# Output projection in the banks of the attention scores, with its buffers and raw weights in other places and half of its first tile among the last heads

## The chip, the core and the metric

The kernel runs on one core of a Trainium2 chip. TensorE multiplies matrices and transposes, and writes only to PSUM, which has 8 banks of 2 KB in each of 128 partitions. VectorE and ScalarE read PSUM; GpSimd works in the on-chip memory (SBUF). Loads are issued by SyncE, most stores by ScalarE. Each engine runs its own instructions in order and waits for the others by semaphores. The metric is device time in microseconds (us).

## The reference

One transformer layer over 256 prompt tokens and 1024 sample tokens of width 1024. Half of the mixing is latent attention with 8 heads, half is attention in a window of the token grid. Both halves are normalised, concatenated and projected; a gated feed-forward part follows.

```python
def encoder_layer(x, ...):
    h = rmsnorm(x, attn_norm_g)
    proj = h @ w_in
    a = mla_group(proj[..., :o1], proj[..., o1:o2], proj[..., o2:o3], ...)
    b = na_group(proj[..., o3:], na_rpb)
    mix = jnp.concatenate([rmsnorm(a, mla_out_g), rmsnorm(b, na_out_g)], axis=-1)
    x = x + mix @ w_o
    h2 = rmsnorm(x, ffn_norm_g)
    x = x + (jax.nn.silu(h2 @ w_gate) * (h2 @ w_up)) @ w_down
    return x
```

All data is fp32. A product is made of three matmuls on numbers split into a high and a low half (`mm3`, lines 108 to 112: L110 high by high, L111 high by low, L112 low by high).

## The kernel before

The 1280 tokens (prompt first) are ten tiles of 128. The stages follow one another: input projection and window attention (to about 360 us), latent attention (to about 688 us), output projection (to about 823 us), the feed-forward products (lines 915 to 1053) and the down projection (from line 1064).

**Latent attention.** `attend` (line 653) is called for four pairs of heads; in a pair the order is the first 256 sample tokens, the prompt, and then the other three blocks of 256 sample tokens (lines 720 to 730). For each head of a block there are two score groups S (L110 to L112) into one of two PSUM tiles of two banks (`s_tile`, in the pools ppa and ppb). VectorE takes the maximum (L681), ScalarE the exponential (L683) into `ex`, TensorE transposes it into `tp` (L689), ScalarE and VectorE split that into a high and a low half, PT (L99, L100), and TensorE multiplies with the values into `o` (L699). `o` is copied to `os` (L703), transposed (L707), copied to `ob` (L709), and GpSimd adds and scales it into `at` (L712, L714), which ScalarE's queue stores to `a_d` (L717). The tiles tp and o have two banks each, in the pool pp.

**Output projection.** Eight pieces of w_o are loaded through the buffers `m` (three of 4 KB), scaled by GpSimd with the gain `gm` (L762) and split into `wo0` to `wo7` (L94, L96). `mix_in(t)` loads a tile of both attention outputs into `m` and the residual into `x`; ScalarE sums the squares (L779), GpSimd scales (L783), and TensorE transposes in two groups of four into one bank, `trm` (L790), which ScalarE and VectorE split into `mT` (L99, L100). `out_proj` makes two halves of 512 columns, 24 matmuls each, into `po`, and VectorE adds each half to x (L801). `ffn_in` stores x, normalises it (L808, L811), transposes it into `trh` or `trm` (L820) and fills the operands of the next stage.

**What sets the order.** The loop at line 897 asks for tile t + 1 before it projects tile t. Loads are queued on SyncE in the order of the program (line 79), so one that waits holds up those behind it. On the other engines the framework lays down the order when the kernel is built, from a simulated run; `tc.issue_after(ins)` puts the instructions of its block behind `ins` on their engine. At line 898 it holds all of tile t + 1's preparation behind the last high half of tile t's mT. Pools are stacks: those of a later stage lie over those that an earlier one has given back, and each tile waits for the tiles that lay in its place. Here that is:

```python
    for nm in ("lc", "lw", "ke", "kp", "qp", "p2", "qA", "lv0"):
    ...
    for x in reversed(lstack):
        x.release()
    ...
    rw, rm, rxm, rt = r3 = [pool(nm) for nm in ("r3w", "r3m", "r3x", "r3t")]
    po = pool("po", space=PSUM)
```

lc holds the latents (cT, 51,200 bytes per partition), lw small weights (13,312), ke and kp the keys of even pairs and of the prompt (16,384 and 4,096), qp the prompt's queries (4,096), and p2 the small tiles of `attend`, `at` first. r3w holds wo (65,536), r3m the three m and small tiles, r3x two x of 4,096, r3t two mT of 8,192. The PSUM pools pp and po begin at bank 0; ppb lies behind pp and ppa at the other end.

Of the kernel before, what the change touches and what calls it, by code (L numbers as in the profile page):

```python
# [11 lines left out]
F32 = mybir.dt.float32  # L12
# [27 lines left out]
def encoder_trunk(ctx: ExitStack, tc: tile.TileContext, x_tm, x_T, g_attn, w_c, w_v, w_qk,  # L40
# [471 lines left out]
    s_count, last_split = [0], [None]  # L512
# [140 lines left out]
    def attend(p, Q, K, c_lo, c_hi, sample, between=None):  # L653
# [6 lines left out]
        for c in range(c_lo, c_hi):  # L660
            at = p2.tile([P, 2, P], F32, name="at", bufs=2)
            for i in range(2):
# [42 lines left out]
                for u in range(2):  # L705
                    us = slice(u * P, (u + 1) * P)
                    nc.tensor.transpose(op[:, us], os_[:, us], ident)  # L707
# [5 lines left out]
                                        op=ALU.add)  # L713
                nc.gpsimd.tensor_tensor(out=at[:, :, i * DH:(i + 1) * DH], in0=ob[:, :, 0],  # L714
# [36 lines left out]
    rw, rm, rxm, rt = r3 = [pool(nm) for nm in ("r3w", "r3m", "r3x", "r3t")]  # L751
    po = pool("po", space=PSUM)
    gm = rm.tile([P, KC], F32, name="gm")
    gf = rm.tile([P, KC], F32, name="gf")
    load(gm, g_mix)
    load(gf, g_ffn)
    wo = []
    for kc in range(KC):
        raw = rm.tile([P, D], F32, name="m", bufs=3)
        load(raw, w_o[kc])  # L760
        wt = rw.tile([P, 2, D], F32R, name=f"wo{kc}")
        nc.gpsimd.tensor_scalar(out=raw, in0=raw, scalar1=gm[:, kc:kc + 1], scalar2=1.0,  # L762
                                op0=ALU.mult, op1=ALU.mult)
        split_w(wt[:, 0], wt[:, 1], raw)
        wo.append(wt)

    def mix_in(t):
# [4 lines left out]
        x = rxm.tile([P, D], F32, name="x", bufs=2)  # L772
        load(x, x_tm[ts_, :])
# [7 lines left out]
        for i in range(2):  # L781
            hs = slice(i * 512, (i + 1) * 512)
            nc.gpsimd.tensor_scalar(out=mn[:, hs], in0=mx[:, hs], scalar1=r[:, i:i + 1],  # L783
                                    scalar2=1.0, op0=ALU.mult, op1=ALU.mult)
        mT = rt.tile([P, 2, KC, P], F32R, name="mT", bufs=2)
# [6 lines left out]
        return mT, x  # L792

    def out_proj(t, mT, x):
        for hf in range(2):
            hs = slice(hf * 512, (hf + 1) * 512)
            ps = po.tile([P, 512], F32, name="po", bufs=2)
            for kc in range(KC):
                last = mm3(ps, mT[:, 0, kc], mT[:, 1, kc], wo[kc][:, 0, hs], wo[kc][:, 1, hs],
                           kc == 0, kc == KC - 1)  # L800
# [93 lines left out]
    pm = [pool("pm0", space=PSUM, side="right")]  # L894
    cur = mix_in(0)
    A0, w0 = ({}, {}), {}
    for t in range(NT):
        with tc.issue_after(last_split[0]):
            nxt = mix_in(t + 1) if t + 1 < NT else None
        if t == 6:  # L900
            for m, i, b in ((1, 0, "11"), (2, 0, "12"), (1, 1, "11")):
                A0[i][b] = load_A(i, 0, b)
                w0[m, i] = operand(A0[i], m)
        if t == 7:
            A0[1]["12"] = load_A(1, 0, "12")
        last_mm = out_proj(t, *cur)
# [411 lines left out]
```

## Time and profile before

| | us |
|---|---|
| median of three runs | 1643.68 (1642.41 to 1643.81) |
| the profiled execution | 1647.12 |
| its span, first to last instruction | 1645.3 |
| TensorE busy in it | 1594.9 |
| VectorE, ScalarE, GpSimd busy | 884.6, 715.5, 660.4 |

The profile is of one execution, recorded on the chip. Engines are called PE (TensorE), PEld (its weight loads), DVE (VectorE), ACT (ScalarE), POOL (GpSimd) and SP (SyncE); SPq and ACTq are the queues that issue DMAs. L801 is line 801 of the kernel. In a timeline a row gives the start, the duration, the engine, the line, the operation, what it writes and reads, how many were merged, and in brackets the engine's idle time before and what ended it. A matmul's duration overlaps with the next one's, so a rate is read from the starts. PEclk is the granted clock of TensorE, 1.00 being full.

### The profile page before, as it was taken

What the parts mean: (1) busy time and instruction counts of PE and PEld (TensorE: products, weight loads), DVE (VectorE), ACT (ScalarE), POOL (GpSimd) and SP (SyncE); (2) the same over time, 40 slices, a digit from 0 to 9 for tenths busy, and PEclk for the clock granted to TensorE, in tenths of its full rate; (3) what the DMA queues carried; (4) which work ended last, traced back from release to release, by engine and by line L of the source; (5) the groups of instructions that cost most, each with busy time, mean ns of one, the idle gap of its engine ahead of it and who ended that gap; (6) DMA issues with size and microseconds to landing.
All of it is one profiled execution on the core that took longest, in us unless ns stands there. A gap on an engine that the chain in (4) does not pass through costs nothing.

```text
span 1645.3 us, 25695 instructions
## 1 busy us (share of the span) xinstructions
PE 1594.9 (97%) x9601; PEld 1449.9 (88%) x9601; DVE 884.6 (54%) x1473; ACT 715.5 (43%) x1478; POOL 660.4 (40%) x823
## 2 busy tenths in 40 slices
PE   7898999999999999899999999999999999999998
PEld 6897889898888888788889999999999998888886
DVE  4655035455677777534275443344443346876676
ACT  5434145455677777534353222322222333443334
POOL 3461425544111119322686656656656652010002
PEclk9999999999999999999999999999999999999999
DMA  6635312234001013233222322322322337843434
GB/s 220 205 107 147 63 37 54 44 108 159 20 19 34 21 30 100 65 115 135 96 73 94 108 89 60 101 87 95 108 89 65 97 104 256 304 149 96 154 101 152
DMA packets 123244, 171.10 MB, mean 104 GB/s; under 512 B 35504, under 2 KB 67120, under 8 KB 123120
## 3 DMA queue, kind: packets, MB, share of 16 engines
q1 hardware_dynamic: 78880, 120.30, 24.0%
q10 hardware_dynamic: 43680, 46.87, 8.2%
q0 software_dynamic: 560, 2.29, 0.3%
q8 instruction: 75, 1.23, 0.3%
q14 instruction: 49, 0.40, 0.1%
HBM read 118.96 MB, written 50.46 MB: 103 GB/s over the span
## 4 chain that ended last, share of the span: by engine, by line
PE 86%; issue 3%; POOL 3%; DVE 2%; ACT 2%; DMA 2%; SPq 0%; ACTq 0%; POOLq 0%; DVEq 0%
PE M L112 10%; PE M L110 10%; PE M L111 10%; PE d L112 5%; PE d L111 5%; PE d L110 5%; PE o L699 3%; PE tp L689 3%; PE na_o L469 2%; PE po L110 2%; PE po L111 2%; PE po L112 2%; PE pj L110 2%; PE pj L112 2%; PE pj L111 2%
## 5 line engine op out<-in xcount | busy, mean ns | idle before, releaser
L111 PE MATMUL M<-S,wc 128*128 128x320 f32 x1056 | 324.8, 309 | 0.0
L110 PE MATMUL M<-S,wc 128*128 128x320 f32 x1056 | 322.1, 310 | 0.5 <-ACT wc L863 0.2
L112 PE MATMUL M<-S,wc 128*128 128x320 f32 x1056 | 313.1, 310 | 3.9 <-POOL wc L864 3.9
L112 PEld LDWEIGHTS M<-S,wc 128*128 128x128 f32 x1056 | 195.4, 188 | 4.5 <-POOL wc L864 4.5
L110 PEld LDWEIGHTS M<-S,wc 128*128 128x128 f32 x1056 | 197.9, 188 | 1.5 <-ACT wc L863 0.9
L111 PEld LDWEIGHTS M<-S,wc 128*128 128x128 f32 x1056 | 198.6, 188 | 0.0
L864 POOL TENSOR_TENSOR wc<-A,wc 128x512 fp32r<-128x512 f32 x86 | 119.7, 1392 | 84.1 <-ACT wc L863 84.0
L939 DVE TENSOR_TENSOR z<-M,z 128x320 f32<-128x320 f32 x120 | 56.9, 488 | 133.1 <-PE M L112 122.7
L863 ACT CAST wc<-A 128x512 fp32r<-128x512 f32 x86 | 53.5, 622 | 164.7 <-PE M L111 146.7
L864 POOL TENSOR_TENSOR wc<-sum,wc 128x512 fp32r<-128x512 f32 x62 | 87.8, 1417 | 87.0 <-ACT wc L863 87.0
L111 PE MATMUL d<-S,S 128*128 128x512 f32 x310 | 120.6, 390 | 0.0
L112 PE MATMUL d<-S,S 128*128 128x512 f32 x310 | 120.1, 390 | 0.0
L110 PE MATMUL d<-S,S 128*128 128x512 f32 x310 | 119.9, 389 | 0.0
L939 DVE TENSOR_TENSOR zB<-M,zB 128x320 f32<-128x320 f32 x100 | 47.6, 488 | 133.1 <-PE M L112 131.8
L100 DVE TENSOR_TENSOR PT<-tp,PT 128x512 fp32r<-128x512 f32 (+1 forms) x144 | 93.0, 658 | 39.4 <-ACT PT L99 37.9
L863 ACT CAST wc<-sum 128x512 fp32r<-128x512 f32 x62 | 38.4, 619 | 144.3 <-PE M L111 98.1
L99 ACT CAST PT<-tp 128x512 fp32r<-128x512 f32 (+1 forms) x144 | 79.2, 565 | 40.2 <-PE tp L689 37.1
L681 DVE TENSOR_REDUCE mm<-S 128x1 f32<-128x1024 f32 (+1 forms) x80 | 84.8, 1062 | 10.6 <-PE S L112 8.9
L983 ACT CAST S<-as 128x640 fp32r<-128x640 f32 x58 | 42.3, 729 | 96.5 <-issue 58.6
L683 ACT ACTIVATE ex<-S,mm 128x1024 f32<-128x1024 f32 (+1 forms) x80 | 79.7, 996 | 7.5 <-DVE mm L681 6.7
L699 PE MATMUL o<-PT,v 128*128 128x256 f32 x544 | 81.0, 288 | 1.2 <-ACT PT L99 1.2
L689 PE MATMUL tp<-ident,ex 128*128 128x128 f32 x544 | 79.5, 274 | 2.1 <-DVE PT L100 1.2
(401 smaller groups left out, 4054.4 us busy)
## 6 DMA issues: line engine op xcount, KB each, us to landing
as<-act_d SPq DMA_DIRECT2D x73, 320.0 KB
w<-in_w_down_dram SPq DMA_DIRECT2D x44, 256.0 KB
act_d<-z ACTq DMA_DIRECT2D x35, 320.0 KB
act_d<-zB ACTq DMA_DIRECT2D x35, 320.0 KB
A<-in_w_gate_dram SPq DMA_DIRECT2D x42, 256.0 KB
A<-in_w_up_dram SPq DMA_DIRECT2D x42, 256.0 KB
x<-in_x_tm_dram SPq DMA_DIRECT2D x20, 512.0 KB
cT_d<-stg ACTq DMA_DIRECT2D x20, 320.0 KB
```

Source lines behind the costliest of these rows:

```text
L99: i = nc.scalar.copy(out=hi, in_=ps)
L100: nc.vector.tensor_sub(out=lo, in0=ps, in1=hi)
L110: nc.tensor.matmul(out, lhsT=sh, rhs=mh, start=first, stop=False, **kw)
L111: nc.tensor.matmul(out, lhsT=sh, rhs=ml, start=False, stop=False, **kw)
L112: return nc.tensor.matmul(out, lhsT=sl, rhs=mh, start=False, stop=last, **kw).ins
L681: nc.vector.reduce_max(out=nm[:, u:u + 1], in_=S, axis=AX.X, negate=True)
L683: nc.scalar.activation(ex, S, AF.Exp, bias=nm[:, u:u + 1], scale=1.0, accum_out=l[:, u:u + 1])
L689: nc.tensor.transpose(tp[:, j], ex[:, kt * P:(kt + 1) * P], ident)
L699: nc.tensor.matmul(oT, lhsT=vv, rhs=pt[s][g][:, j], start=kt == 0 and s == 0, stop=kt == nkt - 1 and s == 1)
L863: i0 = nc.scalar.copy(out=hi, in_=raw)
L864: i1 = nc.gpsimd.tensor_tensor(out=lo, in0=raw, in1=hi, op=ALU.subtract)
L939: nc.vector.tensor_add(out=o, in0=ps, in1=a)
```

## The change

- The PSUM pool po is allocated from the other end, so that its four tiles lie in the banks of the two score tiles instead of those of o and tp. pm0 and pm1, the pools of the next stage, change sides with it, and `product` takes bank 1 - s.
- The pools are stacked in another order: r3w (with gm in it), r3t0 (mT of even tiles), r3m, r3t1 (mT of odd tiles), r3x. `at` is allocated at its first use, behind ob, instead of ahead of all small tiles of `attend`.
- The eight raw pieces of w_o are loaded in pairs into the places of wo4, wo5, wo6 and mT0, which are filled later, instead of through the m buffers.
- `mix_in` is cut into the part up to the scaling, `mix_T` (transposes and split) and `load_x`. x of tile t is loaded in iteration t, behind a and b of tile t + 1.
- For tile 0, the second half's matmuls are put behind the last transposes of os; the first half's are free to go earlier. Tile 1's preparation is no longer held behind tile 0's split.
- At t = 6, three operands of the next stage are put behind the scaling of tile 7.

```diff
-    s_count, last_split = [0], [None]
+    s_count, last_split, last_os = [0], [None], [None]
...
         for c in range(c_lo, c_hi):
-            at = p2.tile([P, 2, P], F32, name="at", bufs=2)
...
-                    nc.tensor.transpose(op[:, us], os_[:, us], ident)
+                    last_os[0] = nc.tensor.transpose(op[:, us], os_[:, us], ident).ins
...
+                if i == 0:
+                    at = p2.tile([P, 2, P], F32, name="at", bufs=2)
...
-    rw, rm, rxm, rt = r3 = [pool(nm) for nm in ("r3w", "r3m", "r3x", "r3t")]
-    po = pool("po", space=PSUM)
-    gm = rm.tile([P, KC], F32, name="gm")
+    rw, rt0, rm, rt1, rxm = r3 = [pool(nm) for nm in ("r3w", "r3t0", "r3m", "r3t1", "r3x")]
+    po = pool("po", space=PSUM, side="right")
+    gm = rw.tile([P, KC], F32, name="gm")
     gf = rm.tile([P, KC], F32, name="gf")
     load(gm, g_mix)
-    load(gf, g_ffn)
     wo = []
-    for kc in range(KC):
-        raw = rm.tile([P, D], F32, name="m", bufs=3)
-        load(raw, w_o[kc])
-        wt = rw.tile([P, 2, D], F32R, name=f"wo{kc}")
-        nc.gpsimd.tensor_scalar(out=raw, in0=raw, scalar1=gm[:, kc:kc + 1], scalar2=1.0,
-                                op0=ALU.mult, op1=ALU.mult)
-        split_w(wt[:, 0], wt[:, 1], raw)
-        wo.append(wt)
+    def load_wo(n, pl, nm):
+        raws = pl.tile([P, 2, D], F32, name=nm)
+        for j in range(2):
+            kc, raw = 2 * n + j, raws[:, j]
+            load(raw, w_o[kc])
+            nc.gpsimd.tensor_scalar(out=raw, in0=raw, scalar1=gm[:, kc:kc + 1], scalar2=1.0,
+                                    op0=ALU.mult, op1=ALU.mult)
+            wt = rw.tile([P, 2, D], F32R, name=f"wo{kc}")
+            split_w(wt[:, 0], wt[:, 1], raw)
+            wo.append(wt)
...
     def mix_in(t):
...
-        x = rxm.tile([P, D], F32, name="x", bufs=2)
-        load(x, x_tm[ts_, :])
...
-            nc.gpsimd.tensor_scalar(out=mn[:, hs], in0=mx[:, hs], scalar1=r[:, i:i + 1],
-                                    scalar2=1.0, op0=ALU.mult, op1=ALU.mult)
+            mixed[0] = nc.gpsimd.tensor_scalar(out=mn[:, hs], in0=mx[:, hs],
+                                               scalar1=r[:, i:i + 1], scalar2=1.0,
+                                               op0=ALU.mult, op1=ALU.mult).ins
-        mT = rt.tile([P, 2, KC, P], F32R, name="mT", bufs=2)
+        return mn
+
+    def mix_T(t, mn):
+        mT = (rt1 if t % 2 else rt0).tile([P, 2, KC, P], F32R, name=f"mT{t % 2}")
         for q in range(2):
             tr = po.tile([P, 4, P], F32, name="trm", bufs=1)
...
-        return mT, x
+        return mT
+
+    def load_x(t):
+        x = rxm.tile([P, D], F32, name="x", bufs=2)
+        load(x, x_tm[t * P:(t + 1) * P, :])
+        return x
...
             ps = po.tile([P, 512], F32, name="po", bufs=2)
-            for kc in range(KC):
-                last = mm3(ps, mT[:, 0, kc], mT[:, 1, kc], wo[kc][:, 0, hs], wo[kc][:, 1, hs],
-                           kc == 0, kc == KC - 1)
+            with ExitStack() as es:
+                if t == 0 and hf:
+                    es.enter_context(tc.issue_after(last_os[0]))
+                for kc in range(KC):
+                    last = mm3(ps, mT[:, 0, kc], mT[:, 1, kc], wo[kc][:, 0, hs],
+                               wo[kc][:, 1, hs], kc == 0, kc == KC - 1)
...
-    pm = [pool("pm0", space=PSUM, side="right")]
-    cur = mix_in(0)
+    pm = [pool("pm0", space=PSUM)]
+    for n, (pl, nm) in enumerate(((rw, "wo4"), (rw, "wo5"), (rw, "wo6"), (rt0, "mT0"))):
+        load_wo(n, pl, nm)
+    cur = mix_T(0, mix_in(0))
+    load(gf, g_ffn)
     A0, w0 = ({}, {}), {}
     for t in range(NT):
-        with tc.issue_after(last_split[0]):
-            nxt = mix_in(t + 1) if t + 1 < NT else None
+        with ExitStack() as es:
+            if t:
+                es.enter_context(tc.issue_after(last_split[0]))
+            nxt = mix_T(t + 1, mix_in(t + 1)) if t + 1 < NT else None
         if t == 6:
             for m, i, b in ((1, 0, "11"), (2, 0, "12"), (1, 1, "11")):
                 A0[i][b] = load_A(i, 0, b)
-                w0[m, i] = operand(A0[i], m)
+                with tc.issue_after(mixed[0]):
+                    w0[m, i] = operand(A0[i], m)
...
-        last_mm = out_proj(t, *cur)
-        ffn_in(t, cur[1])
+        x = load_x(t)
+        last_mm = out_proj(t, cur, x)
+        ffn_in(t, x)
...
-    pm.append(pool("pm1", space=PSUM))
+    pm.append(pool("pm1", space=PSUM, side="right"))
...
-        bank = s if bank is None else bank
+        bank = 1 - s if bank is None else bank
```

More of the change, by code (lines that the diff above doesn't have):

```diff
@@ L749, in encoder_trunk @@
                                              bufs=2) for b in ("11", "12", "21", "22")}
-    rw, rm, rxm, rt = r3 = [pool(nm) for nm in ("r3w", "r3m", "r3x", "r3t")]
-    po = pool("po", space=PSUM)
-    gm = rm.tile([P, KC], F32, name="gm")
+    rw, rt0, rm, rt1, rxm = r3 = [pool(nm) for nm in ("r3w", "r3t0", "r3m", "r3t1", "r3x")]
+    po = pool("po", space=PSUM, side="right")
+    gm = rw.tile([P, KC], F32, name="gm")
     gf = rm.tile([P, KC], F32, name="gf")
     load(gm, g_mix)
-    load(gf, g_ffn)
     wo = []
-    for kc in range(KC):
-        raw = rm.tile([P, D], F32, name="m", bufs=3)
-        load(raw, w_o[kc])
-        wt = rw.tile([P, 2, D], F32R, name=f"wo{kc}")
-        nc.gpsimd.tensor_scalar(out=raw, in0=raw, scalar1=gm[:, kc:kc + 1], scalar2=1.0,
-                                op0=ALU.mult, op1=ALU.mult)
-        split_w(wt[:, 0], wt[:, 1], raw)
-        wo.append(wt)
+    def load_wo(n, pl, nm):
[8 more added lines that the diff above has]
+            wo.append(wt)
+    mixed = [None]
     def mix_in(t):
```

## The prediction

> **What bounds the kernel now.** I read the page's busy times first, then busy time by stretch around the edit, then the TensorE timeline there, then what ScalarE, GpSimd and the load queue did.
>
> ```profile
> span 1645.3 us, 25695 instructions
> ...
> PE 1594.9 (97%) x9601; PEld 1449.9 (88%) x9601; DVE 884.6 (54%) x1473; ACT 715.5 (43%) x1478; POOL 660.4 (40%) x823
> ```
>
> TensorE is busy for 97% of the span, so time can come out only where it stands still or runs at a lower clock. The table of stretches (length, busy time of the engines, granted clock, DMA share, GB/s) finds the place:
>
> ```profile
> core 0: us, PE busy (x) PEld busy (x) DVE busy (x) ACT busy (x) POOL busy (x), PEclk, DMA share, GB/s
> ...
> 620.00:662.00 42.00, 41.45 (x289) 37.27 (x288) 31.39 (x48) 31.85 (x70) 41.36 (x39) 1.00 0.30 96
> 662.00:677.00 15.00, 15.00 (x104) 13.56 (x103) 11.67 (x17) 12.87 (x28) 4.37 (x10) 1.00 0.47 159
> 677.00:691.00 14.00, 9.17 (x68) 7.58 (x67) 5.61 (x10) 7.07 (x16) 2.56 (x6) 0.94 0.06 19
> 691.00:706.00 15.00, 15.00 (x59) 12.03 (x60) 2.87 (x5) 2.40 (x6) 2.25 (x4) 0.83 0.12 36
> 706.00:823.00 117.00, 116.93 (x571) 94.23 (x570) 42.21 (x63) 46.15 (x113) 44.94 (x65) 1.00 0.34 117
> ```
>
> Attention (to 677) and the projection from 706 on leave TensorE no gap. Between them it is busy 9.17 of 14 us, and for the 15 us after that its clock is 0.83. The TensorE timeline (start, us, line, what, and in brackets the idle time before):
>
> ```profile
> 663.64 0.38 PE L707 MATMUL o<-ident,os 128*128 128x128 f32 x2
> 663.85 1.04 PE L689 MATMUL tp<-ident,ex 128*128 128x128 f32 x8
> 664.64 0.48 PE L110 MATMUL S<-mk0o,mq0B 128*128 128x512 f32 x1
> ...
> 666.12 1.56 PE L699 MATMUL o<-PT,v 128*128 128x256 f32 x12
> ...
> 676.88 0.38 PE L707 MATMUL o<-ident,os 128*128 128x128 f32 x2
> 677.09 1.03 PE L689 MATMUL tp<-ident,ex 128*128 128x128 f32 x8
> 678.37 1.70 PE L699 MATMUL o<-PT,v 128*128 128x256 f32 x12 [0.24 <-ACT PT L99]
> 679.90 0.60 PE L689 MATMUL tp<-ident,ex 128*128 128x128 f32 x4
> ...
> 686.28 0.44 PE L707 MATMUL o<-ident,os 128*128 128x128 f32 x2 [0.46 <-ACT os L703]
> 686.56 0.60 PE L790 MATMUL trm<-ident,m 128*128 128x128 f32 x4
> 690.80 0.79 PE L110 MATMUL po<-wo,mT 128*128 128x512 f32 x1 [3.64 <-ACT mT L99]
> ...
> 696.38 0.39 PE L110 MATMUL po<-wo,mT 128*128 128x512 f32 x1
> 696.61 0.40 PE L111 MATMUL po<-wo,mT 128*128 128x512 f32 x1
> ```
>
> The last score matmul is out just before 676.88. What is left is a chain of small steps in which TensorE waits for ScalarE and VectorE again and again. At 686.56 the first four transposes of tile 0 of the projection run, and then nothing for 3.64 us until its matmuls at 690.80. ScalarE says why:
>
> ```profile
> 679.70 0.21 ACT L683 ACTIVATION_READ_ACCUMULATOR ex<-S,mm 128x1 f32 x1
> ...
> 688.17 0.37 ACTq L67 DMA_DIRECT2D a_d<-at  x1
> 690.16 0.58 ACT L99 CAST mT<-trm 128x512 fp32r<-128x512 f32 x1 [3.03 <-DMA a_d<-at]
> ```
>
> The cast into mT waits for the store of the last at tile, though it reads nothing of it: by the tile sizes in the code, the first mT buffer lies over the two at buffers. The lowest wait is thus one for memory, not for data.
>
> **How much is lost there.** I compare with the undisturbed heads. From 663.64 to 676.88 two heads take 13.24 us with no gap. They hold four score groups of six matmuls (664.64 to 666.12, 1.48 us each, 5.92) and one block of eight transposes (663.85 to 664.64, 0.79) beyond what the tail holds, so the tail's own work is 13.24 - 5.92 - 0.79 = 6.53 us. It took from 677.09 to 686.56, 9.47 us: 2.94 lost. Four transposes are half of 0.79, 0.40; from 686.56 to 690.80 are 4.24 us: 3.84 lost. From 690.80 to 696.38 eleven projection matmuls and four transposes run. At the 0.23 us between the last two rows that is 2.53 + 0.40 = 2.93 us against 5.58: 2.65 lost to the lower clock. Together 9.43 us.
>
> **The change, part by part.** *Score banks.* The projection's PSUM tiles move from the banks of o and tp, in use to the end, to those of the two score tiles. The last exponential has read its scores at 679.91 (679.70 + 0.21). From there tile 0 can be transposed and split, 6.65 us before 686.56. Up to 679.90 nothing changes, and 0.49 us (1.28 from 677.09 to 678.37, less 0.79) stays lost.
>
> *mT, x and at elsewhere.* By the sizes, the first mT buffer now lies over the keys of pair 2, the three m buffers over those and small tiles of pair 3, at behind ob. The 3.03 us wait for the store is gone. The x buffer of tile 0 lies over the last exponentials and the os tiles, so its load can go out only after the last os transposes: what comes late next, priced below.
>
> *Half of tile 0 among the heads.* From 679.9 the work is eight transposes (0.79), the 24 matmuls of the first half (24 x 0.23 = 5.52) and the rest of the tail. The tail's dense work to 679.90 is 0.79 for the transposes plus about 1.4 for twelve o matmuls, so 6.53 - 2.2 = 4.3 is left, and 10.6 us of work stands where the chain needed 6.7 (679.90 to 686.56). TensorE has other work in nearly every wait. The first split needs the transposes (0.40), the cast (0.58) and VectorE's low half (as long again); two blocks of tail work, about 1 us, cover most of it. I put 1.0 us for gaps there and 0.5 for order that doesn't quite fit. Then no idle time is long enough to lower the clock, and the second half follows on the last os transposes. Gain: 9.43 - 0.49 - 1.5 = 7.4 us. If every gap closes it is 8.9. If the half doesn't get in among the heads and the transposes don't either, the 2.94 stays and about 1 us of transposes and cast follows the heads: 5.5.
>
> *The clock.* A second gap shows how it answers:
>
> ```profile
> 842.21 0.42 PE L112 MATMUL M<-S,wc 128*128 128x320 f32 x1 [3.30 <-POOL wc L864]
> 842.47 0.31 PE L110 MATMUL M<-S,wc 128*128 128x320 f32 x1
> ...
> 844.70 0.47 PE L110 MATMUL M<-S,wc 128*128 128x320 f32 x1
> ```
>
> Here 3.30 us idle are followed by matmuls at 0.31 and only then by slower ones at 0.47, so the lower clock does not come at a fixed time after the gap. [...] By the rows alone I keep the 2.65 in the sum; without it the gain would be 4.8, a rival below.
>
> *Raw weights in later weights' places.* The work is the same, the time is not:
>
> ```profile
> L94 POOL TENSOR_SCALAR wo<-m x8: 1045/1050/1065, 621.4 to 657.8; 128x1024 fp32r<-128x1024 f32 x8
> L96 POOL TENSOR_TENSOR wo<-m,wo x8: 2407/2424/2433, 623.5 to 659.6; 128x1024 fp32r<-128x1024 f32 x8
> ```
>
> ```profile
> 620.23 1.13 POOL L762 TENSOR_SCALAR m<-m,gm 128x1024 f32<-128x1024 f32 x1
> ```
>
> ```profile
> 590.63 0.30 SPq L76 DMA_DIRECT2D mq1B<-rope_d  x1
> 611.99 0.35 SPq L64 DMA_DIRECT2D gm<-in_g_mix_dram  x1
> ...
> 612.87 34.79 SPq L64 DMA_DIRECT2D m<-in_w_o_dram  x8
> 664.46 0.33 SPq L64 DMA_DIRECT2D m<-a_d  x1
> ```
>
> The eight loads ran from 612.87 through three m buffers. Now gm and the first raws lie where the latents were, so the queue can go on soon after 590.63; only the last pair waits for pair 2's keys, near 612. The splits (1.13 to scale, 1.05 + 2.42 to split: 36.8 us over eight) start about 20 us earlier and end near 640 instead of 662. GpSimd was full in 620 to 662 (41.36 of 42) and TensorE lost only 0.55 us of it; I take 0, and keep 0.55 either way. What it brings is that tile 0 is scaled long before 679.9. mix_in(1) is no longer held back; its squares go onto ScalarE among heads, which was busy 12.87 of 15: up to 0.5, inside the 0.5 above.
>
> *x later in the load queue.* x(t) was loaded a tile ahead; now it stands behind a and b of tile t+1. Rows of the load queue, the adds, and two loads of the same size:
>
> ```profile
> 797.30 0.33 SPq L64 DMA_DIRECT2D m<-a_d  x1
> ```
>
> ```profile
> 705.64 0.69 DVE L801 TENSOR_TENSOR x<-po,x 128x512 f32<-128x512 f32 x1 [1.04 <-PE po L112]
> ...
> 806.81 0.69 DVE L801 TENSOR_TENSOR x<-po,x 128x512 f32<-128x512 f32 x1 [2.71 <-PE po L112]
> ...
> 810.02 0.69 DVE L801 TENSOR_TENSOR x<-po,x 128x512 f32<-128x512 f32 x1 [0.21 <-PE po L112]
> ```
>
> ```profile
> 23.51 6.55 DMA x<-in_x_tm_dram
> ...
> 76.52 4.68 DMA x<-in_x_tm_dram
> ```
>
> a of tile 9 went out at 797.30, so x(8) would at about 798.2 and land by 804.7 at the slower 6.55 us, 2.1 us before its add at 806.81. Cost 0. For tile 0 there is no such lead: last os transposes at about 677.09 + 0.49 + 6.53 + 0.79 + 5.52 = 690.4, load 4.68, add 0.69: 695.8. TensorE wants that bank back after the second half and tile 1's transposes, 690.4 + 5.5 + 0.8 = 696.7. It fits by 0.9 us; at 6.55 it is late by 1.0.
>
> *The rest* has one answer: pm0 and pm1 change sides, and 1 - s gives each half the banks it had; the operands of t = 6 held behind tile 7's scaling concern GpSimd, which is busy 44.94 of 117 there. The next wait, 3.30 at 842.21, is GpSimd's and only moves forward.
>
> The sum against the profiled execution: 1647.12 - 7.4 = 1639.7 (its span is 1645.3). It ran 3.4 us above the median of the three runs, 1643.68; the gain carried over to that gives **1636.3**.
>
> **Rivals.** (1) *x of tile 0.* If the first add stands in VectorE's queue ahead of tile 1's low halves, and tile 1's second transposes stand in the middle of the second half, TensorE stops until 695.8 plus 0.7: up to 3.7 us. For it: the margin of 0.9. Against: nothing else is in the load queue or on the DMA engines then but one small store. Gain 3.7, 1640.0. (2) *No lower clock in the ordinary runs.* They were shorter than the profiled one; but other things differ there too. Gain 4.8, 1638.9. (3) *It doesn't do what it says:* the order written for TensorE leaves projection and transposes behind the heads, waiting on m or weights. Gain 0 to 2, 1642.7. Against: GpSimd is free from 640. (4) *Slower: x a tile late throughout.* Place: the load queue, where x(t) stands behind a load that waits for an m buffer. The add may be late by 2.1 us without notice, and by 810.02 - 806.81 - 0.69 = 2.5 more before the second add is late; from 4.6 us on, each us costs one per tile. At 6.0 us late nine tiles lose 9 x 1.4 = 12.6, less 7.4: 1648.9. Against: m buffers came free by 797.30 with the same three in use.
>
> **How the numbers follow.** Forecast 0.60 (gain 5.5 to 8.9); rival 1 0.12, 2 0.08, 3 0.10, 4 0.10. A change of 0.2% (3.3 us) is about what can be told from none. Faster by more: forecast, rival 2 and two thirds of rival 1, 0.76. Within: 0.04 + 0.10 = 0.14. Slower: 0.10. Range: 1634.0 below (8.9 and the 0.55 give 1634.2) to 1642.2, which leaves out the slower case and the far half of rival 3.
>
> **What would show it.** Right: the first trm transposes near 680, before the last os ones; projection matmuls between tp and o groups; no idle time over 1 us at the join, the clock near 1.00 in 691 to 706; weight splits from about 597; tile 0's second add near 698.2 (705.64 - 7.4). Rival 1: a wait of TensorE around 693 to 697 for mT or x. Rival 4: TensorE idle in every tile from 706 on. The forecast is wrong if the join still shows 3 us idle, or if heads before 677 get gaps that they did not have.

## The result and the profile after

| | before | after |
|---|---|---|
| median | 1642.91 us (1638.84 to 1643.81) | 1632.05 us (1630.35 to 1634.0) |
| ratio | | 0.9935, 95% interval 0.9923 to 0.9946 |
| the profiled execution, its span | 1647.12, 1645.3 us | 1632.26, 1630.4 us |
| TensorE busy in it | 1594.9 us | 1589.9 us |

The change makes the kernel 10.7 us faster (8.9 to 12.7). The forecast was 1636.3, its range began at 1634.0: the direction and the mechanism were right, the size was not.

The page of the changed kernel, its head:

```profile
span 1630.4 us, 25683 instructions
...
PE 1589.9 (98%) x9601; PEld 1447.9 (89%) x9601; DVE 884.4 (54%) x1473; ACT 715.6 (44%) x1478; POOL 663.0 (41%) x823
```

TensorE's busy time fell by 5.0 us of the 14.9 that the span lost; the rest was idle time. The table of stretches of the changed kernel, in the columns shown before: what was 9.17 busy of 14 us and then a clock of 0.83 is now full, at full clock.

```profile
662.00:677.00 15.00, 14.76 (x111) 13.55 (x109) 10.47 (x16) 13.65 (x31) 6.25 (x12) 1.00 0.20 60
677.00:691.00 14.00, 13.97 (x79) 11.82 (x78) 4.45 (x7) 3.93 (x9) 1.72 (x4) 1.00 0.20 68
691.00:698.00 7.00, 7.00 (x34) 5.69 (x33) 2.40 (x4) 2.86 (x7) 2.76 (x6) 1.00 0.60 185
```

The TensorE timeline of the changed kernel at the join of heads and projection (tp is L688 here, os L706, trm L798, and the adds of x are L817):

```profile
672.22 1.04 PE L688 MATMUL tp<-ident,ex 128*128 128x128 f32 x8
673.49 1.70 PE L698 MATMUL o<-PT,v 128*128 128x256 f32 x12 [0.24 <-ACT PT L99]
...
675.95 0.60 PE L688 MATMUL tp<-ident,ex 128*128 128x128 f32 x4
676.38 0.60 PE L798 MATMUL trm<-ident,m 128*128 128x128 f32 x4
676.82 0.38 PE L706 MATMUL o<-ident,os 128*128 128x128 f32 x2
677.04 0.65 PE L688 MATMUL tp<-ident,ex 128*128 128x128 f32 x4
677.71 0.50 PE L110 MATMUL po<-wo,mT 128*128 128x512 f32 x1
678.05 0.39 PE L111 MATMUL po<-wo,mT 128*128 128x512 f32 x1
678.27 0.60 PE L688 MATMUL tp<-ident,ex 128*128 128x128 f32 x4
...
686.49 0.38 PE L706 MATMUL o<-ident,os 128*128 128x128 f32 x2
686.63 0.48 PE L110 MATMUL po<-wo,mT 128*128 128x512 f32 x1
```

Tile 0's first transposes (676.38) and first projection matmuls (677.71) stand between the transposes of the last heads, the second half follows on the last os transposes (686.49) without a gap, and the only idle time is the 0.24 us that the kernel before had there too. ScalarE's casts into mT, tile 0's first and tile 1's first:

```profile
677.07 0.59 ACT L99 CAST mT<-trm 128x512 fp32r<-128x512 f32 x1
...
688.73 0.59 ACT L99 CAST mT<-trm 128x512 fp32r<-128x512 f32 x1 [1.46 <-POOL at L715]
```

Tile 0's no longer waits for the store of at; a wait of 1.46 us for GpSimd's last operation on at is left, at tile 1's, and TensorE doesn't feel it there.

I measure two stretches in every kernel. The **join** runs from the start of the last 24 transposes tp to tile 0's second add of x; the **tiles** from there to the last add. Before: 705.64 - 677.09 = 28.55 us and 823.26 - 705.64 = 117.62. After, by VectorE's adds:

```profile
690.58 0.69 DVE L817 TENSOR_TENSOR x<-po,x 128x512 f32<-128x512 f32 x1 [0.53 <-DMA x<-in_x_tm_dram]
692.42 0.69 DVE L817 TENSOR_TENSOR x<-po,x 128x512 f32<-128x512 f32 x1 [1.15 <-PE po L112]
...
809.13 0.69 DVE L817 TENSOR_TENSOR x<-po,x 128x512 f32<-128x512 f32 x1 [0.21 <-PE po L112]
```

692.42 - 672.22 = 20.20 us and 809.13 - 692.42 = 116.71: 8.35 us from the join, 0.91 from the tiles, 9.26 together. Each stretch repeats within 0.1 us from one profile of a kernel to the next. The spans of the two profiles differ by more, 14.9 us. But 4.87 of that lie ahead of the join (677.09 against 672.22), where the change moves no work: 2.8 of it between the last input projection matmul and the first latent score, which took 41.0 to 46.4 us in the 20 profiles of this study, in changed and unchanged kernels alike, and 2.0 ahead of that. The remaining 0.8 lie behind the last add. So I judge parts by the two stretches, and whole kernels by the ratio of their times.

### The profile page after: what moved, and what is told of

Read it like the earlier page. It is cut to its first block, busy times and chain, and to the rows that moved or that the text cites. A ratio compares the mean times of both kernels' runs of the same rounds, so it can differ in the third digit from the quotient of the medians.

```text
span 1630.4 us, 25683 instructions
## 1 busy us (share of the span) xinstructions
PE 1589.9 (98%) x9601; PEld 1447.9 (89%) x9601; DVE 884.4 (54%) x1473; ACT 715.6 (44%) x1478; POOL 663.0 (41%) x823
## 4 chain that ended last, share of the span: by engine, by line
PE 89%; issue 2%; DMA 2%; POOL 2%; ACT 2%; DVE 2%; SPq 0%; ACTq 0%; POOLq 0%; DVEq 0%
PE M L112 11%; PE M L110 11%; PE M L111 11%; PE d L112 5%; PE d L111 5%; PE d L110 5%; PE o L698 4%; PE tp L688 3%; PE po L110 2%; PE po L111 2%; PE pj L110 2%; PE po L112 2%; PE pj L112 2%; PE pj L111 2%; PE na_o L469 2%
## 5 line engine op out<-in xcount | busy, mean ns | idle before, releaser
L711 POOL TENSOR_TENSOR ob<-ob 128x128 f32<-128x128 f32 x40 | 18.3, 457 | 156.9 <-ACT ob L708 153.7
```

## The experiments

| kernel | join, us | tiles, us | ratio to before |
|---|---|---|---|
| before | 28.55 | 117.62 | 1 |
| before, again | 28.49 | 117.63 | |
| changed | 20.20 | 116.71 | 0.9935 (0.9923 to 0.9946) |
| changed, again | 20.22 | 116.73 | 0.9942 (0.9923 to 0.9960) |
| at at its old place | 22.30 | 116.84 | 0.9958 (0.9945 to 0.9970) |
| no hold for either half | 23.18 | 116.66 | 0.9970 (0.9957 to 0.9982) |
| hold for both halves | 21.22 | 116.58 | 0.9955 (0.9941 to 0.9970) |
| old PSUM banks | 22.88 | 116.78 | 0.9964 (0.9950 to 0.9977) |
| raws in m again | 23.29 | 116.70 | 0.9971 (0.9957 to 0.9985) |
| x a tile ahead again | 19.84 | 124.25 | 0.9977 (0.9964 to 0.9990) |
| before, at late alone | 27.29 | 117.62 | 0.9983 (0.9971 to 0.9995) |
| before, banks alone | 28.04 | 117.64 | 1.0002 (0.9990 to 1.0013) |
| before, idle time filled | 26.10 | 117.63 | 0.9988 (0.9976 to 1.0000) |

Each ratio is to runs of the kernel before that were made beside it. My theory was that of the prediction: the join was long because of a wait for memory, the banks and the lower clock, and the change removes all three. The rivals were that one part carries it all, that the lower clock does not belong to the ordinary runs, and that something outside the join takes part.

**The two kernels again** (e1_before_again, after_again): no edit.

> The kernel before, once more, for a second profile. In the two profiles at hand the join (from the last score matmuls to tile 0's second add) differs by 8.4 us, but the whole span by 14.9: 2.0 us of the difference stand in the first 160 us and 2.8 us between 360 and 398 us, where no edit acts on the order. Theory (chance): these 4.8 us are the profiled execution's own, which ran 4.1 us above the median of before; this profile has its span near 1641, its loads of the last query tiles near 586 instead of 590.6, and the same join: 3.6 us of idle TensorE before the first projection matmul, tile 0's second add about 29 us after the last group of eight exponential transposes starts. Rival (layout): the other place of at among the small tiles makes latent attention start 2.8 us earlier; then this profile shows the same loss between 360 and 398 us as the first one.

> The changed kernel once more, on the chip of the runs beside it. If what its profile showed belongs to the kernel, the join (start of the last 24 transposes of exponentials to tile 0's second add) takes 20.2 us within 0.1 again, matmuls of even tiles follow each other every 227 ns and those of odd tiles every 233, and the time stands 9 to 11 us below the kernel before. If these were chance of one execution, the rates come out equal or exchanged, and the time moves by more than 2 us.

Before came at 1646.29 us in its one run, the changed kernel at 1632.17 (median of six). Join and tiles are those of the first profiles to 0.06 us. They belong to the kernels. The other half of what was expected of e1 missed: its span was 1644.5 us, not near 1641, and from the last input projection matmul to the first latent score it took 45.6 us, about what the first profile took (45.5; the changed kernel 42.7). That is the sign that the rival named. The other profiles settle it: with at at its old place the stretch took 41.2 us (e15) to 45.6, with at behind ob 41.0 (e5) to 46.4 (e16), so it does not go by the place of at.

### Parts taken out of the changed kernel

**at at its old place** (e2_at_first):

```diff
         for c in range(c_lo, c_hi):
+            at = p2.tile([P, 2, P], F32, name="at", bufs=2)
...
-                if i == 0:
-                    at = p2.tile([P, 2, P], F32, name="at", bufs=2)
```

> The changed kernel with at allocated ahead of the other small tiles again, as before. mT of tile 1 then lies over at and must wait for the store of the last one. Theory (banks and half): tile 1 has 5.6 us of second half ahead of it, so a wait of 1 to 2 us at its first cast is covered or nearly so: 0 to 1 us slower than the changed kernel, ratio to before 0.9935 to 0.9942. Rival (memory only: the wait for the store was the whole loss): the wait comes back at tile 1 and costs 3 us or more, ratio 0.9955 or above. Rival (layout at the start of latent attention): the 2.8 us between 360 and 398 us are lost again, and the span up to 590 us is longer by as much than in the changed kernel.

The join grows by 2.1 us, more than the 0 to 1 us of the theory and less than the 3 of the rival (its ratio, 0.9958, lies where the rival put it). In ScalarE's timeline it is now tile 1's cast into mT that waits for the store of at; the second half covers most of that wait, and 1.66 us of it reach TensorE:

```profile
693.51 0.58 ACT L99 CAST mT<-trm 128x512 fp32r<-128x512 f32 x1 [5.33 <-DMA a_d<-at]
```

```profile
694.94 0.65 PE L797 MATMUL trm<-ident,m 128*128 128x128 f32 x4 [1.66 <-DVE mT L100]
```

**Hold for both halves** (e3_no_half):

```diff
-                if t == 0 and hf:
+                if t == 0:
```

> The changed kernel with both halves of tile 0 held behind the last transposes of os; the transposes of tile 0 may still run among the heads. Theory (the half fills the tail): the tail stays 2.4 to 2.9 us longer than its own work, TensorE goes on without idle time after the heads and at full clock, so 2.0 to 3.0 us slower than the changed kernel; ratio to before 0.9948 to 0.9953. Rival (memory only): the half only moves work, and the gain is that of the wait and the clock: within 0.7 us of the changed kernel, ratio 0.9933 to 0.9939.

Tile 0's matmuls all stand behind the last os transposes, yet join and tiles together are only 0.9 us longer (137.80 against 136.91). By the times it is 3.3 us, with intervals of 2 to 3 us; the half among the heads is worth about 1 us by the profile, not the 2 to 3 expected, and more is not shown. Tile 0's transposes and four of tile 1's still stand among the heads here, and no idle time of TensorE there is over 0.26 us.

**Old PSUM banks** (e4_old_banks):

```diff
-    po = pool("po", space=PSUM, side="right")
+    po = pool("po", space=PSUM)
...
-        bank = 1 - s if bank is None else bank
+        bank = s if bank is None else bank
```

(pm0 and pm1 change sides back too.)

> The changed kernel with the projection's PSUM tiles back in the banks of o and tp, and pm0, pm1 and their use as before; buffers, raw weights and the order of loads as changed. Theory (banks): tile 0's transposes stand behind the last transposes of os again, the tail keeps its 2.9 us, and the cast into mT follows the transposes, so TensorE stands still for about 1 us and the clock is not lowered: 3.5 to 4.5 us slower than the changed kernel, ratio to before 0.9957 to 0.9963. Rival (memory only): the banks give nothing, ratio as for the changed kernel, 0.9935.

The join is 2.7 us longer: without the scores' banks nothing of tile 0 gets in among the heads. (By the times it is 4.8 us, with intervals of 2 to 3 us; 3.5 to 4.5 were expected.) The other 5.7 of the 8.35 us are still won: TensorE stands still for 0.68 us behind the transposes instead of 3.64, and the clock stays at 1.00.

**Raws in m again** (e6_raw_in_m): the lines of the kernel before that load w_o come back, load_wo goes.

```diff
+    for kc in range(KC):
+        raw = rm.tile([P, D], F32, name="m", bufs=3)
+        load(raw, w_o[kc])
...
-    for n, (pl, nm) in enumerate(((rw, "wo4"), (rw, "wo5"), (rw, "wo6"), (rt0, "mT0"))):
-        load_wo(n, pl, nm)
```

> The changed kernel, but the eight raw pieces of w_o go one by one through the three m buffers again. In the order written for TensorE, tile 0's transposes and matmuls then all stand behind the last heads. Theory (the raws' new places are what lets tile 0 be scaled in time for the order to put it among the heads): the join takes longer by the heads' lost 2.9 us, less the 0.5 that stays lost either way, and by about 1 us for transposes and cast behind the heads: 23 to 24 us against 20.2, and the time rises by about 3 us. Rival (banks and places of mT and at carry it all): join within 0.7 us of 20.2 and the time that of the changed kernel.

The join is 3.1 us longer, as expected, and the heads ahead of it lose 1.2 us more (276.5 against 275.3 from the first latent score). In GpSimd's timeline the last weight is split at 677.42 and tile 0 scaled only at 681.63, when the last heads are nearly through:

```profile
677.42 2.38 POOL L96 TENSOR_TENSOR wo<-m,wo 128x1024 fp32r<-128x1024 f32 x1
681.63 1.36 POOL L785 TENSOR_SCALAR m<-m,rm 128x512 f32<-128x512 f32 x2
```

**x a tile ahead again** (e8_x_ahead):

```diff
     cur = mix_T(0, mix_in(0))
+    x_cur = load_x(0)
...
             nxt = mix_T(t + 1, mix_in(t + 1)) if t + 1 < NT else None
+            x_nxt = load_x(t + 1) if t + 1 < NT else None
...
-        x = load_x(t)
+        x = x_cur
+        x_cur = x_nxt
```

> The changed kernel with x of tile t + 1 loaded in iteration t, behind tile t + 1's transposes, as early as in the kernel before (tile 0's still ahead of its matmuls). Theory (x's later place in the load queue costs nothing, its adds come in time): from tile 0's second add to the last one it stays at 116.7 us, and the time within 1 us. Rival (the later x delays adds here and there): some tenths of a us per tile are won, 1 to 3 us over ten tiles.

Neither theory saw this: 7.5 us are lost in the tiles, all of it between tile 0 and tile 1 (20.37 us instead of 12.49 from tile 0's second add to tile 1's). The load queue of the changed kernel, and then that of this one (x is tile 0's, a_d tile 1's):

```profile
660.83 0.36 SPq L64 DMA_DIRECT2D m<-a_d  x1
...
686.94 0.33 SPq L64 DMA_DIRECT2D x<-in_x_tm_dram  x1
```

```profile
688.34 0.33 SPq L64 DMA_DIRECT2D x<-in_x_tm_dram  x1
...
689.19 0.43 SPq L64 DMA_DIRECT2D m<-a_d  x1
```

x of tile 0 has to wait for the last os transposes, whose memory it takes. Ahead of tile 1's a and b it holds them back for some 27 us, tile 1 isn't there when TensorE comes to it, and in the TensorE and the stretch view stand the idle time and the low clock behind it (10.82 busy of 15 us, clock 0.77):

```profile
697.45 1.12 PE L836 MATMUL trh<-ident,m 128*128 128x128 f32 x4 [3.68 <-DVE m L827]
```

```profile
691.00:706.00 15.00, 10.82 (x45) 8.41 (x44) 5.59 (x8) 7.27 (x18) 4.08 (x8) 0.77 0.59 189
```

So the new place of x, behind the next tile's a and b, is no price of the change but a condition of it.

**Free half** (e7_free_half): nothing of tile 0 is held.

```diff
-                if t == 0 and hf:
+                if False:
```

> The changed kernel without the hold on tile 0's second half, so that its matmuls stand among the last heads too. Theory (at the join TensorE has no idle time left to fill, so that it matters little which half stands where): the join stays within 0.5 us of 20.2 and the time within 1 us of the changed kernel's. Rival (the hold is needed: matmuls that are put ahead of the last heads' steps delay the last transposes of os, and with them x of tile 0): the join grows by 1 us or more.

The rival is right in the number: the join is 3.0 us longer. More matmuls stand among the heads, and the last os transposes come at 690.03. TensorE's and ScalarE's timelines behind them:

```profile
690.03 0.38 PE L706 MATMUL o<-ident,os 128*128 128x128 f32 x2
...
693.73 0.63 PE L798 MATMUL trm<-ident,m 128*128 128x128 f32 x4 [1.70 <-DVE mT L100]
695.25 0.47 PE L110 MATMUL po<-wo,mT 128*128 128x512 f32 x1 [0.89 <-DVE x L817]
```

```profile
691.87 0.37 ACTq L67 DMA_DIRECT2D a_d<-at  x1
692.28 0.59 ACT L99 CAST mT<-trm 128x512 fp32r<-128x512 f32 x1 [1.46 <-POOL at L715]
```

Behind the last os transposes tile 1's cast must wait for GpSimd's last operation on at (1.46 us), TensorE behind it stands still for 1.70, and then for 0.89 until x of tile 0 has been added from the bank that it wants. The changed kernel has the same 1.46 us on ScalarE, but 24 matmuls of the second half (686.63 to 692.22, 5.6 us) cover it. Work that is brought forward is missing as cover behind; the hold keeps half a tile there.

### Parts done alone in the kernel before

**at late** (e17_before_at_late) is the edit of e2 the other way round; **banks** (e18_before_banks) that of e4.

> The kernel before with at allocated at its first use, behind ob, and nothing else changed. Theory (the wait of the cast for at's store is what stops TensorE at the join): the 3.0 us wait goes, with it nearly all of the 3.64 us without work, and the lower clock behind it: the join falls from 28.5 us by 3 to 5.5, to 23 to 25.5, and the time by as much. Rival (the first mT buffer then lies over another small tile that is used to the end): the wait stays under another name and the join at 28 us or more.

> The kernel before with the projection's PSUM tiles in the banks of the score tiles (and the next stage's pools on the other sides), nothing else changed. Theory (the banks bring nothing as long as the cast into mT waits for the store of at): tile 0's first transposes move ahead of the last os ones, 0.4 us at most are won, the join stays between 28.1 and 28.5 us. Rival (the banks are the larger part by themselves): the join falls by 2 us or more.

ScalarE's first cast into mT, with at late and then with the banks:

```profile
684.75 0.59 ACT L99 CAST mT<-trm 128x512 fp32r<-128x512 f32 x1 [1.50 <-POOL at L715]
```

```profile
688.39 0.58 ACT L99 CAST mT<-trm 128x512 fp32r<-128x512 f32 x1 [3.03 <-DMA a_d<-at]
```

With at late alone, half of the rival holds: the cast still waits, now for GpSimd's last operation on at, the wait shrinks from 3.03 to 1.50 us, and the join by 1.26 instead of 3 to 5.5. The theory also had the lower clock go with the wait, and it didn't. TensorE stands still for 2.11 us instead of 3.64:

```profile
685.38 0.80 PE L110 MATMUL po<-wo,mT 128*128 128x512 f32 x1 [2.11 <-ACT mT L99]
```

That was still followed by half the clock from 684.6 to 691.4 (its row stands at the end of this document). With the banks alone the 3.03 us stay and the join shrinks by 0.5. The two parts alone bring 1.8 us; taken out of the whole they cost 2.1 and 2.7, and the whole brings 8.35. The parts need each other: tile 0 gets in among the heads only where its banks (e4) and its scaled rows (e6) are there early, and each wait that is left sets the time behind.

**Idle time filled** (e10_before_warm): 30 transposes of the identity, read by nobody, are added to the kernel before while it waits for mT.

```diff
+            if t == 0 and q == 0:
+                dm = pm[0].tile([P, 512], F32, name="M0", bufs=4)
+                with tc.issue_after(tl):
+                    for i in range(30):
+                        nc.tensor.transpose(dm[:, 0:P], ident, ident)
```

> The kernel before with 30 transposes of the identity, read by nobody, put behind tile 0's first transposes, so that TensorE is busy for about 3.0 of the 3.64 us in which it waits for the first mT; all else stays. Theory (the lower clock is the answer to the idle time and costs 2.65 us): the matmuls after the wait come at full clock, tile 0's second add comes about 2.6 us earlier (join 25.9 us instead of 28.5), and the time falls by about 2.6 us. Rival (the clock falls for another reason, or does not fall in ordinary runs): the join stays at 28.5 us, or it shrinks in the profile and the time stays.

TensorE's timeline and the stretches:

```profile
681.78 3.44 PE L795 MATMUL M<-ident 128*128 128x128 f32 x30
685.59 0.50 PE L110 MATMUL po<-wo,mT 128*128 128x512 f32 x1 [0.37 <-ACT mT L99]
```

```profile
677.00:691.00 14.00, 12.73 (x85) 10.89 (x83) 3.32 (x5) 4.42 (x11) 3.35 (x8) 1.00 0.04 11
691.00:706.00 15.00, 15.00 (x70) 12.15 (x69) 3.43 (x5) 3.44 (x8) 3.64 (x7) 1.00 0.30 105
```

The wait for mT is as long as before, but the clock stays at 1.00 and the join is 2.45 us shorter, against the 2.65 that the prediction read off the rows. So in this join the lower clock is the answer to the idle time. The time falls by 2.0 us, with an interval of 0 to 3.9: this speaks for the lower clock in the other runs too, but does not show it by itself.

### Where the tiles' 0.9 us come from

Matmuls overlap (0.39 us each, the next one starting 0.23 us later), so I take the distance of 13 successive starts, 12 intervals. The changed kernel in tile 4 and in tile 5:

```profile
735.40 0.39 PE L110 MATMUL po<-wo,mT 128*128 128x512 f32 x1
...
738.12 0.39 PE L111 MATMUL po<-wo,mT 128*128 128x512 f32 x1
...
747.24 0.40 PE L112 MATMUL po<-wo,mT 128*128 128x512 f32 x1
...
750.04 0.40 PE L112 MATMUL po<-wo,mT 128*128 128x512 f32 x1
```

2.72 / 12 = 227 ns in the even tile, 2.80 / 12 = 233 in the odd one; before it is 233 in all ten. Even tiles have mT0, odd ones mT1. The same order of the same work, another address: seven small edits test that. All but one put unused bytes into a pool. The place of mT is given by its distance in bytes per partition from the first weight, by the addresses that the framework gave out; each weight is 8192 bytes, so the others have the same distance modulo 512.

| kernel | edit | distance of mT, modulo 512 | ns | tiles, us |
|---|---|---|---|---|
| before | | 320 and 320 | 233 | 117.62 |
| changed | | 0 (even), 288 (odd) | 227, 233 | 116.71 |
| e5_pad96 | 96 bytes behind gf | 0, 384 | 227, 232 | 116.59 |
| e9_before_pad | 64 bytes behind gf, in before | 384 and 384 | 232 | 117.39 |
| e11_mT0_512 | 512 bytes ahead of mT0 | 0, 288 | 227, 233 | 116.76 |
| e13_mT1_4096 | small tiles ahead of the weights | 0, 0 | 227, 227 | 115.79 |
| e14_pad224 | 224 bytes behind gf | 0, 0 | 227, 227 | 115.66 |
| e15_before_pad192 | 192 bytes behind gf, in before | 0 and 0 | 227 | 115.65 |
| e16_mT0_off32 | 32 bytes ahead of mT0 | 32, 320 | 233, 233 | 117.60 |

```diff
     gf = rm.tile([P, KC], F32, name="gf")
+    rm.tile([P, 56], F32, name="pad")
```

That is e14; e5 has 24 floats there, e9 16 and e15 48 in the kernel before. e11 and e16 have `rt0.tile([P, 128], ...)` and `rt0.tile([P, 8], ...)` ahead of mT0, and e13 puts gf and the small tiles of r3m into a pool of their own ahead of r3w.

> The changed kernel with 96 unused bytes ahead of the m buffers, so that the second mT buffer has the same address modulo 128 as the weights and the first mT buffer. Theory (the spacing of matmuls goes by where the two operands lie relative to each other): matmuls of odd tiles come every 227 ns like those of even tiles, five tiles times 48 matmuls times 6 ns = 1.4 us less from tile 0's second add to the end of the projection, 115.3 us instead of 116.7. Rival (even tiles are faster for another reason, such as the stage's order): 116.7 stays, and the time too.

> The kernel before with 64 unused bytes ahead of the m buffers, so that both mT buffers have the weights' address modulo 128; nothing else is changed. Theory of placement: matmuls of the projection come every 227 ns instead of 233 in all ten tiles, 10 x 48 x 6 ns = 2.9 us less from tile 0's second add to the last, 114.7 us instead of 117.6, and the time falls by about 3 us. Rival: 233 ns and 117.6 us stay, the time is that of the kernel before.

> The changed kernel with 512 unused bytes ahead of the first mT buffer, so that its distance from the weights is no longer a multiple of 8192 bytes (it stays one of 128); the order of all work is the same. Theory (matmuls are 6 ns closer where the halves of both operands lie a multiple of a few KB apart): even tiles slow down from 227 to 233 ns like the odd ones, 116.7 us from tile 0's second add to the last become 117.6. Rival (even tiles are faster for another reason than the address): 227 and 116.7 stay.

> The changed kernel with the projection's small tiles (288 bytes) in a pool ahead of the weights instead of ahead of the m buffers: the weights and the first mT buffer move by 288 bytes together, the second mT buffer keeps its address but now lies 5 x 4096 bytes behind the first; the order of all work is the same. Theory (multiples of 4096 bytes between the operands bring the matmuls closer): odd tiles fall from 233 to 227 ns too, 115.3 us from tile 0's second add to the last instead of 116.7, and the time 1.4 us below the changed kernel. If only multiples of 8192 do, or the address has no part in it, 116.7 stays.

> The changed kernel with 224 unused bytes ahead of the second mT buffer, which brings it to 169 x 512 bytes behind the weights; gf and the small tiles stay where they were. Theory (the two operands a multiple of 512 bytes apart bring the matmuls closer): odd tiles fall from 233 to 227 to 229 ns, from tile 0's second add to the last one it is 115.8 us instead of 116.7, and the time about 0.9 us below the changed kernel. Rival (only multiples of 4096, or the address has no part): 116.7 stays.

> The kernel before with 192 unused bytes ahead of x and the mT buffers, which puts both mT buffers at a multiple of 512 bytes from the weights; nothing else is changed. Theory of placement: all ten tiles fall from 233 to 227 to 229 ns, from tile 0's second add to the last one about 115.6 us instead of 117.6, and the time falls by about 2 us. Rival: 117.4 to 117.6 us as with 64 bytes, and the time of the kernel before.

> The changed kernel with 32 unused bytes ahead of the first mT buffer, so that neither mT buffer is a multiple of 512 bytes from the weights. Theory of placement: even tiles rise from 227 to 233 ns, from tile 0's second add to the last one it is 117.6 us as in the kernel before, and the time about 0.9 us above the changed kernel; the join stays at 20.2 us or a few tenths more. Rival: 116.7 stays.

My first theory (a multiple of 128 bytes is enough) fell with e5 and e9, the second (it takes a multiple of a few KB) with e11, which kept 227 ns at a shift of 512 bytes, and e14. e13 also tells against mT's own address as the cause: mT1 stayed where it was, the weights moved, and the odd tiles went from 233 to 227. What is left holds in all nine kernels: the matmuls come every 227 ns where mT lies a multiple of 512 bytes from the weights, and every 232 or 233 where it doesn't. e16, with both buffers off, has the kernel before's 117.60 again. In e14 tile 5 is as fast as an even one (12 intervals, 2.72 us):

```profile
748.18 0.39 PE L110 MATMUL po<-wo,mT 128*128 128x512 f32 x1
...
750.90 0.39 PE L110 MATMUL po<-wo,mT 128*128 128x512 f32 x1
```

The changed kernel's 0.9 us in the tiles are thus shown: it put mT0 right behind the weights. Whether a smaller unit than 512, such as 256, would do isn't tried.

By the times, e14 is the fastest kernel run: 1630.85 us (1630.54 to 1633.98), ratio 0.9936 (0.9921 to 0.9952). Its 1.05 us in the tiles are clear in the profile; that ratio and the changed kernel's can't be told apart. e5 gave 0.9938, e9 1.0004, e11 0.9940, e13 0.9958, e15 0.9989 and e16 0.9952. In e13 the next stage lost over 4 us, more than the tiles had gained: the order around its first operands came out differently, perhaps since the first of them now lies over gf, which is used to the end. That cause was not tried; e14, which leaves gf in its place, doesn't lose them.

## Why the prediction was right in kind and wrong in size

**The join.** "The lowest wait is thus one for memory, not for data" holds: e17 and e2 move that wait about. The projection got in among the heads, the idle time is gone, the clock is 1.00, in the order foretold. The step that failed is the term "I put 1.0 us for gaps there and 0.5 for order that doesn't quite fit". Of the 9.43 us lost before, 9.43 - 8.35 = 1.08 are still lost; 0.49 of them were named as staying, which leaves 0.6 instead of 1.5. About 0.2 of the difference is not overlap but the closer matmuls told of above: e16, which takes them away, has a join of 20.39 us against 20.20. So gaps and order took about 0.8. The view of after says why: no gap over 0.24 us. I counted two blocks of tail work as cover for the split and then still charged for the gaps. "If every gap closes it is 8.9" was nearer. The fallback of 5.5, with nothing of tile 0 among the heads, is borne out by e4 (5.7). Of the 2.7 us that e4 puts on tile 0's work among the heads, the half itself carries only 0.9 by the profile (e3).

**The tiles.** A second step failed: "mT, x and at elsewhere" was priced by waits alone. That another address changes the rate of the matmuls had no term, and it is 0.9 us in the tiles, besides the 0.2 in the join.

**The base.** The gain was subtracted from a median of three runs, 1643.68; over six it is 1642.91, 0.8 us lower. With 0.9 from the join and 0.9 from the tiles that makes 2.6 of the 4.25 us between 1636.3 and 1632.05. The other 1.7 lie within the interval of the ratio (8.9 to 12.7, and 6.6 to 12.6 for the changed kernel's second set of runs, against 9.26 by the profile); the second set by itself gives 9.5, close to the profile. They were not traced to any part of the kernel and stay open.

**The range.** Its low end, 1634.0, was the best case of the join and 0.55 us more, taken from the median of three. It left out what the rest of the kernel and the spread of the medians could add, each of which was about 1 us.

**The raw weights.** "Weight splits from about 597" was wrong. The loads went out early, but GpSimd's first scaling stands behind a head's at in the order written for it:

```profile
586.67 17.74 SPq L64 DMA_DIRECT2D wo<-in_w_o_dram  x6
```

```profile
615.09 0.40 POOL L715 TENSOR_TENSOR at<-ob,mr 128x128 f32<-128x128 f32 x1
615.47 1.15 POOL L765 TENSOR_SCALAR wo<-wo,gm 128x1024 f32<-128x1024 f32 x1
...
654.14 2.39 POOL L96 TENSOR_TENSOR wo<-mT,wo 128x1024 fp32r<-128x1024 f32 x1
...
665.61 1.37 POOL L787 TENSOR_SCALAR m<-m,rm 128x512 f32<-128x512 f32 x2
```

I moved the splits with their loads and overlooked the order of the engine that makes them. The splits end at 656.53, not near 640. Tile 0 was scaled at 665.61 all the same, 11 us ahead of its transposes, and e6 shows that the part is needed.

**x, and the rivals.** "Cost 0" for the later x was right, the reason was thin: e8 shows that at its old place it would have cost 7.5 us. Rival 1 did not come. x was issued at 686.94 and its add began at 690.58 after a wait for it; TensorE next wrote that bank at 692.57, 1.3 us after the add's end. Without the hold (e7) TensorE does wait for that add, as rival 1 had it, but only 0.89 us; the larger part of the 3.0 us lost there is the wait for memory. Rival 3 fell with the timeline: the projection does stand among the heads. Rival 4 has no support: after the first tile no add waits for x. Rival 2 is made unlikely by the whole: without the lower clock's 2.65 us the two stretches would give 6.6, below the 8.9 to 12.7 measured first and at the edge of the second set's interval; e10 speaks against it as well.

## What to carry to other kernels

Before work can move forward across a stage border, all that it needs there (PSUM banks, buffers, weights, the load queue) must be free early; price the parts together, since each alone may show little, as here (1.26 and 0.5 of 8.35 us). When work is taken from behind a chain of small steps, ask what covered that chain's last waits, and leave enough there (in e7 too little was left, and the join was 3.0 us longer). And a load whose memory comes free late belongs behind those loads that needn't wait (in e8 it stood ahead of them, and 7.5 us were lost).

## What the runs showed of the hardware

- In the nine kernels of the table, the projection's matmuls (128x512) came every 227 ns where the two operands lay a multiple of 512 bytes apart, and every 232 or 233 ns otherwise. In e13 the weights moved and mT1 kept its place, and its tiles went from 233 to 227 ns. The traces can't say where the 6 ns go.
- With transposes in the idle time the clock stayed up: 30 of them in e10, and the granted clock was 1.00 from 677 to 706. That shows only that transposes kept the full clock here, not that they would bring it back.
- The lower clock did not come at a fixed time after the idle time began, and did not last equally long. Both in the kernel before and in e15 TensorE waits 3.64 us for mT, from 687.16 to 690.80 and from 679.18 to 682.82. The clock is half from 689.4 to 696.2 in the one, and only from 682.3 to 685.7 in the other: it falls 2.2 and 3.1 us after the wait began, and stays low for 6.8 against 3.4 us. The join of e15 is 1.4 us shorter, of which its closer matmuls explain about 0.3 (48 times 6 ns). Rows of the kernel before, of e15 and of e17 (the clock is the number ahead of the last two):

```profile
687.20:689.30 2.10, 0.00 (x0) 0.00 (x0) 0.00 (x0) 0.00 (x0) 0.85 (x2) 1.00 0.10 30
689.50:696.10 6.60, 5.30 (x15) 4.23 (x16) 1.38 (x2) 2.40 (x6) 0.34 (x2) 0.50 0.02 4
696.30:703.00 6.70, 6.70 (x32) 5.44 (x32) 0.00 (x0) 0.00 (x0) 1.71 (x3) 1.00 0.25 78
```

```profile
682.40:685.60 3.20, 2.78 (x9) 2.29 (x10) 0.69 (x1) 0.37 (x1) 0.00 (x0) 0.50 0.03 5
685.80:692.60 6.80, 6.80 (x31) 5.61 (x31) 0.69 (x1) 1.80 (x5) 2.25 (x4) 1.00 0.18 55
```

```profile
684.60:691.30 6.70, 5.92 (x16) 4.75 (x17) 1.38 (x2) 2.40 (x6) 0.89 (x2) 0.50 0.08 22
```

What followed a gap of the same length thus differed. Idle times of 2.11 us (e17) and of 3.30 us (the prediction's second gap; the clock was 0.50 from 844 to 846) were also followed by the lower clock. Idle times of 1.66 us (e2) and 1.70 us (e7), a little later in the join, were not: the projection matmuls behind them come every 0.23 us, against 0.43 at half the clock in e15 and e17. What sets the time at which the clock falls was not shown.
